# Linear attention: one norm for the outputs of two chunks, and a scaling by two factors

## The chip, the cores and the metric

The kernel runs on one core of a Trainium2 chip. The metric is the device time of one execution in microseconds. Engines are named as in the profile: PE (TensorE) multiplies matrices, DVE (VectorE) and ACT (ScalarE) work element by element, POOL (GpSimd) makes masks, and SP (SyncE) issues nearly all transfers.

## The reference, cut to what matters

One layer of a decoder step: a shared input projection, a stick-breaking attention group, a gated linear attention group, SiLU gates, an output projection and residual norms, for a prompt of 16 + 1024 tokens and 8 samples of 4 tokens with paged keys and values. The change lies in the linear attention group, whose output of 256 columns per head is normed by token before its gate:

```python
def rms_norm(x, g):
    xf = x.astype(jnp.float32)
    var = jnp.mean(xf * xf, axis=-1, keepdims=True)
    return (xf * lax.rsqrt(var + EPS) * g.astype(jnp.float32)).astype(x.dtype)
...
    o_gla = rms_norm(o_gla, gla_norm_g)
    o_gla = o_gla.transpose(0, 2, 1, 3).reshape(B, L, GLA_WIDTH)
...
    mixed = jnp.concatenate([o_sb * jax.nn.silu(sg), o_gla * jax.nn.silu(gg)], axis=-1)
```

## The kernel before

The input projection is the spine of the program. `inproj` makes 128 columns of it at a time, for all tokens in three pieces, as three matmuls for each of 16 slices (a high and a low half of both operands): `acc_gk` is such a projection, of the keys of a linear attention head. Other work is written as Python generators and woven in: `inproj` calls `W.beat()` after every six matmuls, and a beat lets each generator whose delay has run out (`W.spawn(generator, delay)`, `yield n`) write its next instructions. One beat is about 1 us of matmuls. The tile framework's scheduler then sets each engine's order from this sequence and its own estimates; at run time each engine takes its queue strictly in that order and waits on semaphores.

The four heads ("groups") of the linear attention run in turn, from about 900 to 1460 us. `chunks` goes through nine chunks of 128 tokens (the ninth has 16), two beats apart. For each chunk TensorE makes `U`, the chunk's part of the state, and `o`, its output, partly from the last state `S`; VectorE updates `S`; ScalarE copies `o` to the tile `ow` and squares it, with the row sums in `ssq`. Then `chunk_out` is spawned. It calls `rstd_` for 1/sqrt of the mean square: `v` on VectorE, an estimate `r` by logarithm and exponential on ScalarE, one Newton correction `t` in three VectorE steps, and `r*t` in a fourth. VectorE scales `ow` by that; three beats later TensorE transposes the two halves of `ow` into one PSUM tile `otr`, ScalarE copies each half to `gst` with the norm's gain, and SP writes each to DRAM (`od`) for the gate to read later.

Between these stand, on the same engines: `decay` of the next head (tiles `al`, `ny`, `e`, `cb`; not for the last head), the split of the projection's weights (`wr` to `wh` on ScalarE and `wl` on VectorE), and `z_feed`, the samples' attention logits on VectorE: four `jk` instructions for each page `kp` of cached keys, two beats apart, with pages fetched up to six ahead on SP's queue. SP's queue holds the `od` writes, the pages, and the weights.

The staging tiles (`stage`) rotate over seven buffers, the tiles `U`, `o` and `otr` have one PSUM buffer each, and `ssq` three small ones.

Of the kernel before, what the change touches and what calls it, by code (L numbers as in the profile page):

```python
# [10 lines left out]
F32 = mybir.dt.float32  # L11
# [4 lines left out]
AF = mybir.ActivationFunctionType  # L16
ALU = mybir.AluOpType
# [3 lines left out]
P = 128  # L21
# [12 lines left out]
DV = 256  # L34
# [48 lines left out]
def hybrid_step(ctx: ExitStack, tc: tile.TileContext, x_prompt, x_sample, cache_k, cache_v, state_gla,  # L83
# [5 lines left out]
    vec, act, pool = nc.vector, nc.scalar, nc.gpsimd  # L89
# [17 lines left out]
    W = Weaver()  # L107

    def stage(nm, dt=F32):
        return stg.tile([P, 384], dt, tag="stg", name=nm)  # L110
# [41 lines left out]
    td = [dram.tile([P, 8, 1024], F32, name=f"td{j}") for j in range(4)]  # L152
    sd = [[dram.tile([P, 512], F32, name=f"sd{j}_{k}") for k in range(8)] for j in range(2)]

    def rstd_(pl, ssq, n, rows, w, nm):

        v = pl.tile([P, w], F32, tag="rs_v", name=f"v_{nm}")
        r = pl.tile([P, w], F32, tag="rs_r", name=f"r_{nm}")
        t = pl.tile([P, w], F32, tag="rs_t", name=f"t_{nm}")
        v, r, t = v[:rows], r[:rows], t[:rows]  # L160
        vec.tensor_scalar(v, ssq, 1.0 / n, EPS, ALU.mult, ALU.add)
        act.activation(r, v, AF.Ln)
        act.activation(r, r, AF.Exp, scale=-0.5)
        vec.tensor_tensor(t, r, r, ALU.mult)
        vec.tensor_tensor(t, t, v, ALU.mult)
        vec.tensor_scalar(t, t, -0.5, 1.5, ALU.mult, ALU.add)
        vec.tensor_tensor(r, r, t, ALU.mult)
        return r

# [22 lines left out]
    with tc.tile_pool(name="xp", bufs=2) as xp, tc.tile_pool(name="xps", bufs=5, space=PSUM) as xps:  # L192
# [57 lines left out]
        for c, (lo, hi) in enumerate(CHUNKS):  # L250
            n = hi - lo
# [401 lines left out]
    with tc.tile_pool(name="gp", bufs=1) as gp, tc.tile_pool(name="gps", bufs=1, space=PSUM) as gps:  # L653
# [11 lines left out]
        def view(t, off, *dims):  # L665
            a = t if isinstance(t, bass.AP) else t[:]
            return bass.AP(tensor=a.tensor, offset=a.offset + off, ap=[list(a.ap[0])] + [list(d) for d in dims])

        def col(c):

            return EB * (1 - c % 2) + c // 2 * P

        def slot(c):

            return 8 if c == 8 else 4 * (1 - c % 2) + c // 2
# [204 lines left out]
                yield 1  # L880
                packed(rep, pv[:, f * P:(f + 1) * P], 1, f"v{g}_{f}")

        def chunk_out(g, c, rows, ow, ssq):

            r = rstd_(gp, ssq[:rows], DV, rows, 1, f"g{g}_{c}")
            vec.tensor_scalar(ow[:rows, :DV], ow[:rows, :DV], r, None, ALU.mult)
            yield 3
            ps = gps.tile([P, DV], F32, tag="tr", name=f"otr{g}_{c}")
            st = stage(f"gst{g}_{c}")
            s0 = META if c == 0 else 0  # L890
            for f in range(2):
                nc.tensor.transpose(ps[:, f * P:f * P + rows], ow[:rows, f * P:(f + 1) * P], ident[:rows, :rows])
                src = view(ps, f * P + P - 1, (-1, P)) if c % 2 else ps[:, f * P:f * P + rows]
                act.activation(st[:, f * P:f * P + rows], src, AF.Copy, scale=gnrm[:, f:f + 1])
                nc.sync.dma_start(od[8 + 2 * g + f][:, c * P + s0 - META:c * P + rows - META], st[:, f * P + s0:f * P + rows])

        def samples_out(g, ow, ssq):

            r = rstd_(gp, ssq[:, 0:2], DV, P, 2, f"g{g}_s")
            for i in range(2):  # L900
                vec.tensor_scalar(ow[i], ow[i], r[:, i:i + 1], None, ALU.mult)
            yield 9
            ps = gps.tile([P, 512], F32, tag="tr", name=f"otr{g}_s")
            st = stage(f"gst{g}_s")
            for i in range(2):
                for f in range(2):
                    nc.tensor.transpose(ps[:, (2 * i + f) * P:(2 * i + f + 1) * P], ow[i][:, f * P:(f + 1) * P], ident[:])
            for f in range(2):
                act.activation(view(st, f * NSMP, (16, 2), (NT, 4), (1, NT)), view(ps, f * P, (2 * P, 2), (32, 4), (1, NT)),
                               AF.Copy, scale=gnrm[:, f:f + 1])  # L910
                nc.sync.dma_start(od[8 + 2 * g + f][:, SEQ:TOUT], st[:, f * NSMP:(f + 1) * NSMP])

        def chunks(g, at, qt, gv, pv, res):

            kd, ebl, pk = res["kd"], res["ebl"], res["pk"]
            S = None
            Ss = {}

            def load_state(b):
                Ss[b] = gp.tile([P, DV], F32, tag="Sb", bufs=4, name=f"Sb{g}_{b}")  # L920
                nc.sync.dma_start(Ss[b][:], state_gla[0, b, g])

            for c in range(9):
                last = c == 8
                rows = 16 if last else P
                ow = stage(f"ow{g}_{c}")
                ssq = gp.tile([P, 2], F32, tag="ssq", bufs=3, name=f"gssq{g}_{c}")
                U = gps.tile([P, DV], F32, tag="U", name=f"U{g}_{c}")
                for f in range(2):
                    mm(U[:, f * P:(f + 1) * P], kd[:rows, c * P:(c + 1) * P], gv[f][:rows, c * P:(c + 1) * P], start=True, stop=True)  # L930
                o = gps.tile([P, DV], F32, tag="o", name=f"o{g}_{c}")
                for f in range(2):
                    oh = o[:rows, f * P:(f + 1) * P]
                    mm(oh, at[:rows, slot(c), :rows], gv[f][:rows, c * P:(c + 1) * P], start=True, stop=(S is None))
                    if S is not None:
                        mm(oh, qt[:, col(c):col(c) + rows], S[:, f * P:(f + 1) * P], start=False, stop=True)
                Sn = gp.tile([P, DV], F32, tag="S", bufs=2, name=f"S{g}_{c}")
                if S is None:
                    act.copy(Sn[:], U[:])
                else:  # L940
                    vec.scalar_tensor_tensor(Sn[:], S[:], ebl[:, c:c + 1], U[:], ALU.mult, ALU.add)
                S = Sn
                act.copy(ow[:rows, :DV], o[:rows])
                act.activation(o[:rows], ow[:rows, :DV], AF.Square, accum_out=ssq[:rows, 0:1])
                W.spawn(chunk_out(g, c, rows, ow, ssq[:, 0:1]), 1)
                if c in (3, 4, 5, 6):
                    load_state(c - 3)
                yield 2
            nc.sync.dma_start(new_state_prompt[0, 0, g], S[:])

            os_ = gps.tile([P, 2, DV], F32, tag="o", name=f"os{g}")
            for f in range(2):
                for i in range(2):
                    for j in range(4):
                        b = 4 * i + j
                        mm(os_[32 * j:32 * j + 32, i, f * P:(f + 1) * P], at[:48, 8, 16 + NT * b:48 + NT * b],
                           gv[f][:48, 8 * P:9 * P], start=(f == 0 and i == 0), stop=False, skip_group_check=True)
            for b in range(NB):
                if b % 4 == 0:
                    for j in range(4):  # L960
                        n = REAL + NT * (b + j)
                        mm(os_[32 * j:32 * j + 32, b // 4, :], qt[:, n:n + 32], Ss[b + j][:], start=False, stop=True,
                           skip_group_check=True)
                Sb = Ss.pop(b)
                km = stg.tile([96, 384], F32R, tag="stg", name=f"km{g}_{b}")[:, :P]
                vec.tensor_scalar(km, pk[:].bitcast(F32), rmask[:, b:b + 1], None, ALU.mult)
                yield 2
                U = gps.tile([P, DV], F32, tag="U", name=f"Us{g}_{b}")
                mm(U[:], km, pv[:], start=True, stop=True)
                sn = stage(f"sn{g}_{b}")[:, :DV]  # L970
                vec.scalar_tensor_tensor(sn, Sb[:], ebl[:, 9 + b:10 + b], U[:], ALU.mult, ALU.add)
                nc.sync.dma_start(new_state_sample[0, b, g], sn)
                if b + 4 < NB:
                    load_state(b + 4)
            ssq = gp.tile([P, 2], F32, tag="ssq", bufs=3, name=f"gssq{g}_s")
            ow = [stage(f"ow{g}_s{i}")[:, :DV] for i in range(2)]
            for i in range(2):
                act.copy(ow[i], os_[:, i, :])
                act.activation(os_[:, i, :], ow[i], AF.Square, accum_out=ssq[:, i:i + 1])
            W.spawn(samples_out(g, ow, ssq), 1)  # L980
# [7 lines left out]
        for g in range(GH):  # L988
# [30 lines left out]
            if g + 1 < GH:  # L1019
                start_decay(g + 1)  # L1020
            W.spawn(chunks(g, at, qt, gv, pv, res), 4)
        for g in range(3, 5):
            gate_group(g)
# [183 lines left out]
    with ExitStack() as out:  # L1207
# [124 lines left out]
        ssq = op.tile([P, 8, 8], F32, tag="yssq", bufs=1, name="yssq")  # L1332
# [238 lines left out]
```

## Time and profile before

| | |
|---|---|
| runs of the kernel before | 2106.34, 3647.29, 2102.87 us (median 2106.34) |
| profiled execution | 2099.06 us, span 2097.3 us |
| granted TensorE clock over the span | 0.997 |
| instructions in the span | 42175 |
| DMA | 301.87 MB, mean 144 GB/s |

The profile is of one execution. The span goes from its first to its last instruction; the execution's own time is 1.8 us longer. Busy times by engine overlap, so they don't add up to the span. A line number such as L886 is that of the kernel before.

### The profile page before, as it was taken

What the parts mean: (1) busy time and instruction counts of PE and PEld (TensorE: products, weight loads), DVE (VectorE), ACT (ScalarE), POOL (GpSimd) and SP (SyncE); (2) the same over time, 40 slices, a digit from 0 to 9 for tenths busy, and PEclk for the clock granted to TensorE, in tenths of its full rate; (3) what the DMA queues carried; (4) which work ended last, traced back from release to release, by engine and by line L of the source; (5) the groups of instructions that cost most, each with busy time, mean ns of one, the idle gap of its engine ahead of it and who ended that gap; (6) DMA issues with size and microseconds to landing.
All of it is one profiled execution on the core that took longest, in us unless ns stands there. A gap on an engine that the chain in (4) does not pass through costs nothing.

```text
span 2097.3 us, 42175 instructions
## 1 busy us (share of the span) xinstructions
PE 2053.5 (98%) x12546; PEld 1865.4 (89%) x12546; DVE 1561.0 (74%) x6372; ACT 962.4 (46%) x2315; POOL 81.2 (4%) x298
## 2 busy tenths in 40 slices
PE   6999999999999999999999999999999999999998
PEld 4999999999999999999899898998988898777776
DVE  7368888889888989898888888887543347453576
ACT  7345555565655556433525335243433325342342
POOL 0000000101000000020000000000000000000000
PEclk9999999999999999999999999999999999999999
DMA  6255554545555442433332433334766675342485
GB/s 203 82 138 153 137 151 136 168 129 152 146 154 141 141 123 77 142 93 78 100 105 78 117 84 101 98 82 140 248 225 229 223 231 190 131 158 73 131 280 187
DMA packets 374912, 301.87 MB, mean 144 GB/s; under 512 B 46489, under 2 KB 315193, under 8 KB 374681
## 3 DMA queue, kind: packets, MB, share of 16 engines
q1 hardware_dynamic: 372488, 298.90, 47.9%
q8 instruction: 99, 1.62, 0.3%
q14 instruction: 133, 1.08, 0.2%
q10 hardware_dynamic: 2192, 0.27, 0.1%
HBM read 241.75 MB, written 57.31 MB: 143 GB/s over the span
## 4 chain that ended last, share of the span: by engine, by line
PE 85%; DVE 7%; DMA 4%; ACT 2%; issue 2%; SPq 0%; DVEq 0%; ACTq 0%; POOL 0%
PE acc_g L292 6%; PE acc_g L293 6%; PE acc_g L294 6%; PE b L1478 4%; PE b L1479 4%; PE b L1480 4%; PE acc_k L292 3%; PE acc_k L293 3%; PE acc_k L294 3%; PE acc_q L292 3%; PE acc_v L292 3%; PE acc_q L293 3%; PE acc_q L294 3%; PE acc_v L294 3%; PE acc_v L293 3%; PE acc_gv L292 2%
## 5 line engine op out<-in xcount | busy, mean ns | idle before, releaser
L393 DVE SCALAR_TENSOR_TENSOR jk<-kp,qb 128x128 f32<-128x128 f32 x2048 | 592.1, 289 | 42.6 <-DMA qb<-qsd 1.7
L292 PE MATMUL acc_g<-hT,wh_g 128*128 128x368 f32 (+2 forms) x768 | 251.2, 327 | 0.0
L293 PE MATMUL acc_g<-hT,wh_g 128*128 128x368 f32 (+2 forms) x768 | 247.2, 322 | 0.0
L294 PE MATMUL acc_g<-hT,wl_g 128*128 128x368 f32 (+2 forms) x768 | 247.0, 322 | 0.0
L1478 PE MATMUL b<-ring,f 128*128 128x512 f32 x416 | 165.3, 399 | 2.7 <-ACT b L1351 1.4
L1316 DVE TENSOR_TENSOR ring<-wr,ring 128x512 fp32r<-128x512 f32 x104 | 70.6, 690 | 129.9 <-ACT ring L1315 129.7
L393 DVE DVE_READ_ACCUMULATOR jk<-kp,qb 128x1 f32 x2048 | 166.3, 81 | 0.0
L1479 PE MATMUL b<-ring,f 128*128 128x512 f32 x416 | 162.6, 391 | 0.7 <-DVE ring L1316 0.7
L1480 PE MATMUL b<-ring,f 128*128 128x512 f32 x416 | 162.2, 390 | 0.0
L292 PEld LDWEIGHTS acc_g<-hT,wh_g 128*128 128x128 f32 x768 | 144.3, 188 | 12.3 <-issue 10.6
L293 PEld LDWEIGHTS acc_g<-hT,wh_g 128*128 128x128 f32 x768 | 144.5, 188 | 0.7
L294 PEld LDWEIGHTS acc_g<-hT,wl_g 128*128 128x128 f32 x768 | 144.3, 188 | 0.8 <-issue 0.8
L1315 ACT CAST ring<-wr 128x512 fp32r<-128x512 f32 x104 | 64.4, 621 | 157.3 <-DMA wr<-in_w_out_dram 74.9
L292 PE MATMUL acc_gv<-hT,wh_gv 128*128 128x384 f32 (+1 forms) x384 | 129.9, 338 | 0.0
L292 PE MATMUL acc_k<-hT,wh_k 128*128 128x378 f32 (+1 forms) x384 | 127.6, 332 | 0.0
L293 PE MATMUL acc_k<-hT,wh_k 128*128 128x378 f32 (+1 forms) x384 | 125.4, 326 | 0.0
L292 PE MATMUL acc_q<-hT,wh_q 128*128 128x368 f32 (+2 forms) x384 | 125.3, 326 | 0.0
L294 PE MATMUL acc_k<-hT,wl_k 128*128 128x378 f32 (+1 forms) x384 | 125.2, 326 | 0.0
L294 PE MATMUL acc_gv<-hT,wl_gv 128*128 128x384 f32 (+1 forms) x384 | 124.6, 325 | 0.0
L293 PE MATMUL acc_gv<-hT,wh_gv 128*128 128x384 f32 (+1 forms) x384 | 124.5, 324 | 0.0
L293 PE MATMUL acc_q<-hT,wh_q 128*128 128x368 f32 (+2 forms) x384 | 123.6, 322 | 0.0
L294 PE MATMUL acc_q<-hT,wl_q 128*128 128x368 f32 (+2 forms) x384 | 123.5, 322 | 0.0
(441 smaller groups left out, 5314.5 us busy)
## 6 DMA issues: line engine op xcount, KB each, us to landing
kp<-in_cache_k_dram SPq DMA_DIRECT2D x512, 64.0 KB
vr<-in_cache_v_dram SPq DMA_DIRECT2D x64, 512.0 KB
tf<-in_w_out_dram SPq DMA_DIRECT2D x64, 256.0 KB
td<-tf SPq DMA_DIRECT2D x64, 256.0 KB
qb<-qsd SPq DMA_DIRECT2D x64, 256.0 KB
wr_g<-in_w_in_dram SPq DMA_DIRECT2D x64, 256.0 KB
wr<-td SPq DMA_DIRECT2D x64, 256.0 KB
wr<-in_w_out_dram SPq DMA_DIRECT2D x48, 256.0 KB
```

What stands on the lines that cost most here:

```text
L292: mm(acc[c][:, :n], wh, hh[k][:, lo:hi], start=(k == 0), stop=False)
L293: mm(acc[c][:, :n], wh, hl[k][:, lo:hi], start=False, stop=False)
L294: W.mark = mm(acc[c][:, :n], wl, hh[k][:, lo:hi], start=False, stop=(k == NK - 1)).ins
L393: ins = vec.scalar_tensor_tensor(jk[:], kp[:], 1.0, qbs[h, b][:, t, :], ALU.mult, ALU.mult, accum_out=zt[:, t, NPG - 1 - i:NPG - i])
L1315: act.copy(wh, r)
L1316: vec.tensor_tensor(wl, r, wh.bitcast(F32), ALU.subtract)
L1478: mm(bk[:], ah, wh, start=first and k == 0, stop=False, skip_group_check=True)
L1479: mm(bk[:], ah, wl, start=False, stop=False, skip_group_check=True)
L1480: mm(bk[:], al, wh, start=False, stop=last and k == 7, skip_group_check=True)
```

## The change

The generator `chunk_out` becomes two functions. The sums of squares of an even chunk and the odd one after it lie side by side in one `ssq` tile. After the odd chunk (and after the ninth, alone) `chunks_out` is spawned: `rstd_` works on both columns at once, and hands back its estimate `r` and correction `t` without multiplying them. Each chunk's `ow` is scaled by both in one instruction. Two beats later the even chunk's transposes, copies and writes are written, and two beats after that the odd one's; they stood three beats after each chunk's own scaling.

```diff
-    def rstd_(pl, ssq, n, rows, w, nm):
+    def rstd_(pl, ssq, n, rows, w, nm, parts=False):
...
         vec.tensor_scalar(t, t, -0.5, 1.5, ALU.mult, ALU.add)
+        if parts:
+            return r, t
         vec.tensor_tensor(r, r, t, ALU.mult)
         return r
...
-        def chunk_out(g, c, rows, ow, ssq):
-
-            r = rstd_(gp, ssq[:rows], DV, rows, 1, f"g{g}_{c}")
-            vec.tensor_scalar(ow[:rows, :DV], ow[:rows, :DV], r, None, ALU.mult)
-            yield 3
+        def chunks_out(g, group, ssq):
+
+            rows, n = group[0][1], len(group)
+            r, t = rstd_(gp, ssq[:rows, :n], DV, rows, n, f"g{g}_{group[0][0]}", True)
+            for i, (c, _, ow) in enumerate(group):
+                vec.tensor_scalar(ow[:rows, :DV], ow[:rows, :DV], r[:, i:i + 1], t[:, i:i + 1], ALU.mult, ALU.mult)
+            for c, _, ow in group:
+                yield 2
+                chunk_out(g, c, rows, ow)
+
+        def chunk_out(g, c, rows, ow):
+
             ps = gps.tile([P, DV], F32, tag="tr", name=f"otr{g}_{c}")
...
-                ssq = gp.tile([P, 2], F32, tag="ssq", bufs=3, name=f"gssq{g}_{c}")
+                if c % 2 == 0:
+                    ssq, group = gp.tile([P, 2], F32, tag="ssq", bufs=3, name=f"gssq{g}_{c}"), []
+                group.append((c, rows, ow))
...
-                act.activation(o[:rows], ow[:rows, :DV], AF.Square, accum_out=ssq[:rows, 0:1])
-                W.spawn(chunk_out(g, c, rows, ow, ssq[:, 0:1]), 1)
+                act.activation(o[:rows], ow[:rows, :DV], AF.Square, accum_out=ssq[:rows, c % 2:c % 2 + 1])
+                if c % 2 or last:
+                    W.spawn(chunks_out(g, group, ssq), 1)
```

The scheduler moves other instructions around this. Names in the rows below end in the chunk's number and a buffer's; all are of the first group. Line numbers of the changed kernel differ by a few.

On TensorE, before, from the first transpose of chunk 0 (`otr_0`) to the projection after chunk 2:

```order
L892 MATMUL otr_0_17624<-ident,ow_0_17495 128x128
L930 MATMUL U_2_17634<-gv_0_16389,kd_17336 128x128
L930 MATMUL U_2_17634<-gv_1_16877,kd_17336 128x128
L934 MATMUL o_2_17637<-gv_0_16389,at_16386 128x128
L892 MATMUL otr_0_17624<-ident,ow_0_17495 128x128
L936 MATMUL o_2_17637<-S_1_17571,gq_15971 128x128
L934 MATMUL o_2_17637<-gv_1_16877,at_16386 128x128
L936 MATMUL o_2_17637<-S_1_17571,gq_15971 128x128
L292 MATMUL acc_gk_2_17404<-hT_150,wh_gk_1_17577 128x304
```

And with the change, from the end of chunk 2's output on:

```order
L947 MATMUL o_2_17617<-S_1_17559,gq_15971 128x128
L294 MATMUL acc_gk_2_17404<-hT_150,wh_gk_1_17565 128x304
L295 MATMUL acc_gk_2_17404<-hT_150,wh_gk_1_17565 128x304
L296 MATMUL acc_gk_2_17404<-hT_150,wl_gk_1_17566 128x304
L294 MATMUL acc_gk_2_17404<-hT_151,wh_gk_1_17565 128x304
L295 MATMUL acc_gk_2_17404<-hT_151,wh_gk_1_17565 128x304
L296 MATMUL acc_gk_2_17404<-hT_151,wl_gk_1_17566 128x304
L901 MATMUL otr_0_17652<-ident,ow_0_17495 128x128
L294 MATMUL acc_gk_0_17402<-hT_152,wh_gk_1_17565 128x384
L295 MATMUL acc_gk_0_17402<-hT_152,wh_gk_1_17565 128x384
L296 MATMUL acc_gk_0_17402<-hT_152,wl_gk_1_17566 128x384
L901 MATMUL otr_0_17652<-ident,ow_0_17495 128x128
```

The two transposes of chunk 0 moved from ahead of and within chunk 2's matmuls to six projection matmuls behind them, and three matmuls stand between them.

On VectorE, before, chunk 0's norm from its first step to the scaling:

```order
L161 TENSOR_SCALAR v_g_0_17532<-gssq_0_17496 128x1
L393 SCALAR_TENSOR_TENSOR jk_5_6_1_17526,zt_5_17250<-kp_5_6_17277,qb_5_17034 128x128
L393 SCALAR_TENSOR_TENSOR jk_5_6_2_17528,zt_5_17250<-kp_5_6_17277,qb_5_17034 128x128
L164 TENSOR_TENSOR t_g_0_17534<-r_g_0_17533 128x1
L393 SCALAR_TENSOR_TENSOR jk_5_6_3_17530,zt_5_17250<-kp_5_6_17277,qb_5_17034 128x128
L165 TENSOR_TENSOR t_g_0_17534<-t_g_0_17534,v_g_0_17532 128x1
L166 TENSOR_SCALAR t_g_0_17534<-t_g_0_17534 128x1
L167 TENSOR_TENSOR r_g_0_17533<-r_g_0_17533,t_g_0_17534 128x1
L886 TENSOR_SCALAR ow_0_17495<-ow_0_17495,r_g_0_17533 128x256
```

And with the change, the norm of chunks 0 and 1, and what stands ahead of it:

```order
L747 TENSOR_TENSOR e_0_17541<-ny_0_17540,e_0_17541 128x384
L395 SCALAR_TENSOR_TENSOR jk_5_7_2_17590,zt_5_17250<-kp_5_7_17308,qb_5_17034 128x128
L753 SCALAR_TENSOR_TENSOR cb_17400<-ones,e_0_17541 128x128 x3
L395 SCALAR_TENSOR_TENSOR jk_5_7_3_17592,zt_5_17250<-kp_5_7_17308,qb_5_17034 128x128
L161 TENSOR_SCALAR v_g_0_17595<-gssq_0_17496 128x2
L952 SCALAR_TENSOR_TENSOR S_2_17622<-S_1_17559,ebl_17195,U_2_17614 128x256
L164 TENSOR_TENSOR t_g_0_17597<-r_g_0_17596 128x2
L165 TENSOR_TENSOR t_g_0_17597<-t_g_0_17597,v_g_0_17595 128x2
L166 TENSOR_SCALAR t_g_0_17597<-t_g_0_17597 128x2
L890 TENSOR_SCALAR ow_0_17495<-ow_0_17495,r_g_0_17596,t_g_0_17597 128x256
L890 TENSOR_SCALAR ow_1_17550<-ow_1_17550,r_g_0_17596,t_g_0_17597 128x256
```

The norm's first step moved behind the decay's maximum (`e_0`), its three scans (`cb`) and the page's last `jk`, and the update of `S_2` stands between it and the correction.

On ScalarE, before, around the copies of chunk 2's transposes (`gst_2`):

```order
L894 ACTIVATE gst_2_17768<-otr_2_17767,gnrm 128x128
L943 COPY ow_4_17775<-o_4_17780 128x256
L743 ACTIVATE e_1_17758<-e_1_17758 128x384
L894 ACTIVATE gst_2_17768<-otr_2_17767,gnrm 128x128
L744 ACTIVATE e_1_17758<-e_1_17758 128x384
L944 ACTIVATE o_4_17780,gssq_4_17776<-ow_4_17775 128x256
```

And with the change:

```order
L954 COPY ow_4_17743<-o_4_17748 128x256
L745 ACTIVATE e_1_17734<-e_1_17734 128x384
L955 ACTIVATE o_4_17748,gssq_4_17744<-ow_4_17743 128x256
L746 ACTIVATE e_1_17734<-e_1_17734 128x384
L903 ACTIVATE gst_2_17791<-otr_2_17790,gnrm 128x128 x2
```

The copies moved behind the decay's exponential and logarithm (`e_1`) and the square of chunk 4, and stand together.

## The prediction

> **What bounds the kernel now.** I read the page first: busy time by engine, the 40 slices, and the chain that ended last.
>
> ```profile
> span 2097.3 us, 42175 instructions
> PE 2053.5 (98%) x12546; PEld 1865.4 (89%) x12546; DVE 1561.0 (74%) x6372; ACT 962.4 (46%) x2315; POOL 81.2 (4%) x298
> PE   6999999999999999999999999999999999999998
> DVE  7368888889888989898888888887543347453576
> PE 85%; DVE 7%; DMA 4%; ACT 2%; issue 2%; SPq 0%; DVEq 0%; ACTq 0%; POOL 0%
> ```
>
> TensorE is busy in 2053.5 of 2097.3 us. All that could be won by freeing other engines is its idle time, 2097.3 - 2053.5 = 43.8 us, which is 2.1% of the span, and that is spread over the whole program. Then the stretches in which the four groups' chunk outputs are made, as busy time by stage, and what TensorE waits for from 980 to 1460 us.
>
> ```profile
> 998.70:1031.30 32.60, 32.60 (x232) 30.71 (x231) 28.14 (x151) 22.48 (x74) 0.00 (x0) 1.00 0.31 84
> 1128.50:1161.20 32.70, 32.70 (x237) 30.82 (x238) 28.16 (x153) 22.48 (x75) 0.00 (x0) 1.00 0.30 84
> 1258.30:1291.00 32.70, 32.70 (x234) 30.82 (x233) 27.88 (x152) 22.25 (x74) 0.00 (x0) 1.00 0.31 84
> 1388.40:1419.90 31.50, 31.50 (x229) 29.93 (x227) 22.03 (x135) 19.03 (x64) 0.00 (x0) 1.00 0.35 87
> PE os L962 <- DMA Sb<-in_state_gla_dram: 1.0, 1, 1.0
> PE tr_v L867 <- DVE pk L859: 0.6, 3, 0.3
> ```
>
> The columns are the stretch, its length, then busy time of PE, weight loads, VectorE, ScalarE. TensorE has no gap in any of the four; VectorE is at 28.14 of 32.60 us (86%), in the last at 22.03 of 31.50 (70%). In 480 us the view lists 1.6 us of waits on TensorE, none of them for the scaled output `ow`. So work taken off VectorE or ScalarE here buys nothing by itself; the change can only cost, where it makes `ow` late for the transposes, which stand in TensorE's queue ahead of projection matmuls.
>
> **What is removed.** The steps of one norm, from the groups by tile (count, then least, median and greatest ns):
>
> ```profile
> L161 DVE TENSOR_SCALAR v_g<-gssq x36: 142/153/155, 1000.9 to 1418.9; 128x1 f32<-128x1 f32 x32, 16x1 f32<-16x1 f32 x4
> L162 ACT ACTIVATE r_g<-v_g x36: 183/203/207, 1001.1 to 1419.1; 128x1 f32<-128x1 f32 x32, 16x1 f32<-16x1 f32 x4
> L167 DVE TENSOR_TENSOR r_g<-r_g,t_g x36: 141/159/160, 1002.2 to 1420.2; 128x1 f32<-128x1 f32 x32, 16x1 f32<-16x1 f32 x4
> L886 DVE TENSOR_SCALAR ow<-ow,r_g x36: 334/353/356, 1002.4 to 1420.5; 128x256 f32<-128x256 f32 x32, 16x256 f32<-16x256 f32 x4
> L167 DVE TENSOR_TENSOR r_g_s<-r_g_s,t_g_s x4: 156/157/157, 1057.8 to 1447.6; 128x2 f32<-128x2 f32 x4
> L941 DVE SCALAR_TENSOR_TENSOR S<-S,ebl,U x32: 468/474/481, 1003.9 to 1416.5; 128x256 f32<-128x256 f32 x32
> ```
>
> Nine norms a group become five (four pairs and the last chunk). Per group that is 4 x 4 small VectorE steps fewer (v, t, t, t) and 9 fewer of L167: 25, in four groups 100; at 0.155 us they are 15.5 us. ScalarE loses 4 x 2 x 4 = 32 steps of 0.203 us, 6.5 us. A step two columns wide costs what one column does (157 against 159 ns), so pairing adds nothing. The scaling by two factors is not in this trace. It lies between L886 with one factor (0.353) and L941, which reads two tensors and a factor (0.474); 36 x 0.12 = 4.3 us if it were the latter. I take 0.353, the same kind of instruction. On VectorE the balance is -11 to -15.5 us, and all of it goes to the end at nothing: the projection matmuls cover it. If that cover were gone, 15.5 us would be 0.7%.
>
> **What is moved.** An even chunk's norm now starts only when the odd chunk's sum of squares is there, and its transposes move by one beat (about 1 us). Whether TensorE waits is worked out on the first pair of the first group, from the times in order of the three engines. I quote the old places and lay the new order over their spacing.
>
> ```profile
> 1003.87 0.53 ACT L743 ACTIVATE e<-e 128x384 f32<-128x384 f32 x1 [0.16 <-DVE e L742]
> 1004.30 0.37 ACT L944 ACTIVATE o<-ow 128x256 f32<-128x256 f32 x1
> 1004.70 0.51 ACT L744 ACTIVATE e<-e 128x384 f32<-128x384 f32 x1
> 1005.23 0.27 PE L892 MATMUL otr<-ident,ow 128*128 128x128 f32 x1
> 1005.24 0.56 DVE L745 TENSOR_TENSOR e<-ny,e 128x384 f32<-128x384 f32 x1
> 1005.34 0.61 PE L930 MATMUL U<-gv,kd 128*128 128x128 f32 x4
> 1005.60 0.37 ACT L894 ACTIVATE gst<-otr,gnrm 128x128 f32<-128x128 f32 x1
> 1005.72 0.28 DVE L393 SCALAR_TENSOR_TENSOR jk<-kp,qb 128x128 f32<-128x128 f32 x1
> 1005.78 0.39 PE L934 MATMUL o<-gv,at 128*128 128x128 f32 x2
> 1005.93 1.05 DVE L751 TENSOR_TENSOR_SCAN cb<-ones,e 128x128 f32<-128x128 f32 x3
> 1006.02 0.33 PE L892 MATMUL otr<-ident,ow 128*128 128x128 f32 x1
> 1006.18 0.39 PE L936 MATMUL o<-S,gq 128*128 128x128 f32 x2
> 1006.77 0.39 PE L292 MATMUL acc_gk<-hT,wh_gk 128*128 128x304 f32 x1
> 1006.90 0.13 DVE L164 TENSOR_TENSOR t_g<-r_g 128x1 f32<-128x1 f32 x1
> 1006.95 0.47 DVE L941 SCALAR_TENSOR_TENSOR S<-S,ebl,U 128x256 f32<-128x256 f32 x1
> 1007.52 0.15 DVE L166 TENSOR_SCALAR t_g<-t_g 128x1 f32<-128x1 f32 x1
> 1007.69 0.34 PE L292 MATMUL acc_gk<-hT,wh_gk 128*128 128x384 f32 x1
> 1007.90 0.35 DVE L886 TENSOR_SCALAR ow<-ow,r_g 128x256 f32<-128x256 f32 x1
> ```
>
> When TensorE wants it: without the transpose of 1005.23 the matmuls of U start there; U takes 0.44 (1005.34 to 1005.78), the output matmuls 0.99 less the 0.16 of the transpose among them (1005.78 to 1006.77), the six `acc_gk` 0.92 (1006.77 to 1007.69). 1005.23 + 0.44 + 0.83 + 0.92 = 1007.42: there stands the first transpose now.
>
> When it is ready: VectorE now has the maximum of the decay (L745 before), a `jk`, three scans and a `jk` ahead of the norm's first step. L745 waits for ScalarE's logarithm (1004.70 + 0.51). In the new order the square comes behind that logarithm, which may so come earlier by one ScalarE step (1004.70 - 1004.30 = 0.40), or not. Earliest 1004.84. From there by the old spacing: 0.48 to the `jk`, 0.21 to the scans, 0.97 to their end, 0.33 for the second `jk` with its hand-over: the norm's first step at +1.99. That step and the two on ScalarE take 0.15 + 2 x 0.20, with three hand-overs about 0.67, an estimate, while S passes; then three steps of 0.19 (1007.52 to 1007.90 is two) and the scaling's 0.35. 1004.84 + 1.99 + 0.67 + 0.57 + 0.35 = 1008.42. TensorE waits 1.0 us, with the later logarithm 1.4. Bounds: nothing, if the queue is 1 us quicker than its old spacing, and 1.5. I take 1.0. What waits behind it are the `acc_gk` matmuls of every projection, so it is time on the path.
>
> Second halves: the second transpose must wait for ScalarE's copy of the first, 1006.02 - 1005.23 = 0.79 after it. Now only three matmuls stand between for chunks 0 and 3 (0.11 + 3 x 0.17 = 0.63, wait 0.16), four for 1 and 4 (0.75, wait 0.04): 0.4 us a group. For chunks 2 and 5 the copy stands on ScalarE behind the decay's exponential and logarithm (0.53, 0.51): 0.2 each, 0.4 a group. For chunk 6 the scaling stands behind the next group's level steps on VectorE: 0.3. Sum for a group: 1.0 + 0.4 + 0.4 + 0.3 = 2.1 us, bounds 0 and 4. The last group has no decay ahead and a VectorE with 30% room; I take 0.4 there. Total 3 x 2.1 + 0.4 = 6.7 us. Today's waits could shrink, by 1.6 us at most as the rows above have it; I leave that out of the sum.
>
> The moved writes of the outputs go past `kp` loads on SP's queue. Their cover is that pages are asked for six ahead, each worth four `jk` of 0.28 and four reads of their sums:
>
> ```profile
> L393 DVE DVE_READ_ACCUMULATOR jk<-kp,qb 128x1 f32 x2048 | 166.3, 81 | 0.0
> ```
>
> 4 x 0.36 = 1.4 us a page, and over 8 us in six. I price this at nothing; the third rival says what it costs without that cover.
>
> **The sum.** The profiled execution took 2099.06 us (span 2097.3). 2099.06 + 6.7 = 2105.8. The undisturbed runs shown are 2102.87 and 2106.34 (the latter the median), 3.8 and 7.3 above the profiled one; +6.7 on their middle, 2104.6, gives 2111. I predict **2111 us**, 0.2% over the median: no change that can be told. About 2% is what a measurement of this kernel can tell.
>
> **Rivals.** *The waits do not arise* (0.26). VectorE is freed of 3.9 us a group, and if its queue gains on TensorE by more than the 1 us that the moved norm needs, the transposes find `ow` ready, as all do today. Against: what is freed lies partly behind the new place. Time: 2104.6 less the waits of 1.6 us, 2103.
>
> *TensorE loses its clock* (0.04), the slower side. The trace has one wait that was followed by half speed:
>
> ```profile
> 908.28 0.44 PE L292 MATMUL acc_gq<-hT,wh_gq 128*128 128x384 f32 x1 [2.64 <-ACT gk L681]
> 909.49 0.53 PE L294 MATMUL acc_gq<-hT,wl_gq 128*128 128x384 f32 x1
> 909.81 0.53 PE L292 MATMUL acc_gq<-hT,wh_gq 128*128 128x384 f32 x1
> 905.00:930.00 25.00, 21.52 (x124) 20.77 (x123) 24.04 (x119) 8.64 (x17) 2.22 (x4) 0.93 0.30 83
> ```
>
> After 2.64 us of waiting matmuls start 0.32 apart instead of 0.17, and the granted clock of the stretch is 0.93: 7% of 25 us, 1.7 us. If each of the twelve pairs of three groups waited so long, it would be 12 x (2.64 + 1.7) = 52 us: 2157. It decides from 2.6 us a pair; my longest wait is 1.5. [...]
>
> *SP's queue holds the pages* (0.08). A `kp` load behind a late output write would stop VectorE for a page (1.4 us) in each of twelve pairs, and S and `ow` behind it: 17 us more, 2128. For it: the writes wait for ScalarE's copies. Against: the lead of six pages.
>
> **How the numbers follow.** Forecast 0.62, rivals 0.26, 0.04, 0.08. Faster by over 2% needs nearly all of TensorE's 43.8 us: 0.01, for what I do not see. Slower by over 2% is the clock's case and a little of the queue's: 0.05. Within 2%: 0.94. The range goes from the first rival less the runs' spread (the profiled one lay 5.5 us under their middle) to the third rival with the runs' spread above: 2098 to 2131 us.
>
> **What would show it.** Right: `PE otr` waiting for VectorE's `ow` at the first chunk of pairs in three groups, about 1 us each, and no such wait in the last group; stretches of the four groups 1 to 4 us longer; 100 VectorE and 32 ScalarE steps gone; the scaling at 0.35. Wrong: no waits at all; a granted clock below 1 in those stretches; `jk` waiting for `kp`; or a scaling near 0.47.

## The result and the profile after

The changed kernel takes 2112.08 us, the median of 7 runs (2108.31 to 2116.33); the kernel before takes 2106.15, the median of 7. The ratio is 1.0034, with a 95% interval of 1.0019 to 1.0049: about 7 us slower (4 to 10). One of the seven runs before took 3647.29 us; the ratio leaves it out. Forecast were 2111 us and a difference below 2%. The profiled execution took 2116.33 us, the longest of the seven.

The page's first lines after, and the chain that ended last by engine:

```profile
span 2114.6 us, 42018 instructions
PE 2064.1 (98%) x12546; PEld 1867.7 (88%) x12546; DVE 1555.5 (74%) x6272; ACT 956.1 (45%) x2283; POOL 80.5 (4%) x298
PE 82%; DVE 8%; DMA 5%; ACT 2%; issue 2%; SPq 0%; DVEq 0%; ACTq 0%; POOL 0%
```

VectorE has 6372 - 6272 = 100 steps fewer and ScalarE 2315 - 2283 = 32, as worked out, yet the span is 17.3 us longer than that of before. Not all of this belongs to the change: where the first group begins, the order of the instructions is still the same on every engine, and the trace is 5.26 us behind there already. Profiled executions differ by that much by themselves (in the first-group rows below this group begins anywhere from 997.06 to 1003.96), so the comparison has to be made group by group. Each row below is one group, from a projection matmul ahead of its first chunk to one behind its samples; the ends are chosen so that both kernels have the same matmuls between them (425, 427, 429, 490). The columns are the stretch, its length, busy time and count of PE, weight loads, VectorE, ScalarE, GpSimd, then the granted clock, DMA share and GB/s. Before:

```profile
998.70:1060.00 61.30, 61.30 (x425) 55.45 (x425) 53.23 (x275) 32.45 (x101) 0.23 (x2) 1.00 0.36 101
1128.50:1190.00 61.50, 61.50 (x427) 55.68 (x427) 53.32 (x278) 32.41 (x101) 0.24 (x2) 1.00 0.37 101
1258.30:1320.00 61.70, 61.70 (x429) 55.89 (x429) 53.23 (x278) 32.22 (x100) 0.24 (x2) 1.00 0.36 102
1388.40:1460.00 71.60, 70.64 (x490) 64.76 (x489) 55.64 (x308) 35.44 (x106) 0.58 (x2) 1.00 0.44 121
```

and after:

```profile
1003.96:1066.98 63.02, 62.43 (x425) 54.94 (x425) 51.06 (x249) 30.92 (x93) 0.24 (x2) 1.00 0.35 98
1135.49:1198.78 63.29, 62.70 (x427) 55.23 (x427) 51.23 (x252) 30.93 (x93) 0.24 (x2) 1.00 0.35 98
1267.09:1330.83 63.74, 62.98 (x429) 55.43 (x429) 51.10 (x252) 30.75 (x92) 0.24 (x2) 1.00 0.35 98
1399.50:1473.85 74.35, 72.59 (x490) 64.83 (x489) 52.61 (x272) 33.55 (x97) 0.37 (x2) 0.98 0.40 114
```

VectorE is busy some 2.1 us less in each of the first three groups, and TensorE takes 1.72, 1.79, 2.04 and 2.75 us longer: 8.30 us together. This fits the 7 us of the timed runs. TensorE's waits in the four groups:

```profile
PE os L974 <- DMA Sb<-in_state_gla_dram: 1.9, 2, 1.8
PE otr L901 <- DVE ow L890: 1.8, 3, 0.6
PE tr_v L869 <- DVE pk L861: 1.0, 4, 0.6
```

The second row was not there before: three waits of 0.6 us for `ow`, one in each of the first three groups. The first row was there with 1.0 us; it comes back below.

The first pair of the first group, in order of time, from all engines:

```profile
1009.27 0.53 ACT L746 ACTIVATE e<-e 128x384 f32<-128x384 f32 x1
1009.83 0.56 DVE L747 TENSOR_TENSOR e<-ny,e 128x384 f32<-128x384 f32 x1 [0.22 <-ACT e L746]
1010.52 1.05 DVE L753 TENSOR_TENSOR_SCAN cb<-ones,e 128x128 f32<-128x128 f32 x3
1011.68 0.16 DVE L161 TENSOR_SCALAR v_g<-gssq 128x2 f32<-128x2 f32 x1
1012.35 0.16 DVE L164 TENSOR_TENSOR t_g<-r_g 128x2 f32<-128x2 f32 x1
1012.53 0.30 PE L296 MATMUL acc_gk<-hT,wl_gk 128*128 128x304 f32 x1
1012.94 0.74 DVE L890 TENSOR_SCALAR ow<-ow,r_g,t_g 128x256 f32<-128x256 f32 x2
1013.41 0.33 PE L901 MATMUL otr<-ident,ow 128*128 128x128 f32 x1 [0.59 <-DVE ow L890]
1013.93 0.34 PE L296 MATMUL acc_gk<-hT,wl_gk 128*128 128x384 f32 x1
1014.20 0.33 PE L901 MATMUL otr<-ident,ow 128*128 128x128 f32 x1
```

The norm's first step stands behind the decay's scans, as the order of the program said. TensorE's last matmul ahead of the transpose starts at 1012.53; these narrower matmuls start 0.14 apart, so the transpose was due at 1012.67 and starts at 1013.41: 0.74 us lost from start to start. Two steps of the norm by tile, with least, median and greatest ns:

```profile
L890 DVE TENSOR_SCALAR ow<-ow,r_g,t_g x36: 396/408/416, 1012.9 to 1432.1; 128x256 f32<-128x256 f32 x32, 16x256 f32<-16x256 f32 x4
L161 DVE TENSOR_SCALAR v_g<-gssq x20: 136/169/172, 1011.7 to 1430.5; 128x2 f32<-128x2 f32 x16, 16x1 f32<-16x1 f32 x4
```

The scaling by two factors takes 0.408 us where that by one took 0.353.

### The profile page after: what moved, and what is told of

Its sections match the earlier page's. It is cut to its first block, busy times and chain, and to the rows that moved or that the text cites. A ratio compares the mean times of both kernels' runs of the same rounds, so it can differ in the third digit from the quotient of the medians.

```text
span 2114.6 us, 42018 instructions
## 1 busy us (share of the span) xinstructions
PE 2064.1 (98%) x12546; PEld 1867.7 (88%) x12546; DVE 1555.5 (74%) x6272; ACT 956.1 (45%) x2283; POOL 80.5 (4%) x298
## 4 chain that ended last, share of the span: by engine, by line
PE 82%; DVE 8%; DMA 5%; ACT 2%; issue 2%; SPq 0%; DVEq 0%; ACTq 0%; POOL 0%
PE acc_g L294 5%; PE acc_g L295 5%; PE acc_g L296 5%; PE b L1490 4%; PE b L1491 4%; PE b L1492 4%; PE acc_k L294 3%; PE acc_k L295 3%; PE acc_k L296 3%; PE acc_v L294 3%; PE acc_q L294 3%; PE acc_q L295 3%; PE acc_q L296 3%; PE acc_v L295 3%; PE acc_v L296 3%; PE acc_gv L294 2%
```

## The experiments

The theory (A): the loss comes from where the paired norm and its transposes stand, and nothing comes back for the steps saved. The rivals are in each expectation. Every ratio below is to the kernel before, run on the same chip.

### The two halves of the change

The scaling by two factors alone, each chunk with its own norm and at its old place:

```diff
-            r = rstd_(gp, ssq[:rows], DV, rows, 1, f"g{g}_{c}")
-            vec.tensor_scalar(ow[:rows, :DV], ow[:rows, :DV], r, None, ALU.mult)
+            r, t = rstd_(gp, ssq[:rows], DV, rows, 1, f"g{g}_{c}", True)
+            vec.tensor_scalar(ow[:rows, :DV], ow[:rows, :DV], r, t, ALU.mult, ALU.mult)
```

(`rstd_` has the flag `parts` as in the change.)

> The scaling by two factors alone: each chunk has its own norm as before, only r*t is left out and the scaling takes r and t. Theory A (the loss comes from where the paired norm and the transposes stand): the order of the transposes is that of before, TensorE waits nowhere for ow, VectorE has 36 steps fewer and each scaling takes 0.41 instead of 0.35 us; time within 1 us of before, ratio 1.000. Rival B (the loss comes with the form of the scaling): ratio 1.002 to 1.0035.

Measured: 0.9994 (0.9985 to 1.0003). Its first and last group:

```profile
1002.80:1063.92 61.12, 61.05 (x425) 55.26 (x425) 52.22 (x266) 32.76 (x101) 0.24 (x2) 1.00 0.39 102
1392.23:1464.72 72.49, 70.94 (x490) 64.77 (x489) 54.92 (x296) 35.92 (x106) 0.81 (x3) 1.00 0.43 119
```

The first group is 0.18 us shorter than before, with 1.0 us less work on VectorE. The form of the scaling cost nothing, and the microsecond saved on VectorE bought less than 0.2 here. The pairing alone, with `r*t` multiplied out:

```diff
-            r, t = rstd_(gp, ssq[:rows, :n], DV, rows, n, f"g{g}_{group[0][0]}", True)
+            r = rstd_(gp, ssq[:rows, :n], DV, rows, n, f"g{g}_{group[0][0]}")
...
-                vec.tensor_scalar(ow[:rows, :DV], ow[:rows, :DV], r[:, i:i + 1], t[:, i:i + 1], ALU.mult, ALU.mult)
+                vec.tensor_scalar(ow[:rows, :DV], ow[:rows, :DV], r[:, i:i + 1], None, ALU.mult)
```

> The pairing alone: r*t is multiplied out for two columns, the scaling takes one factor. Theory A: like the whole change, ratio 1.003 to 1.004. ow comes 0.19 later for the added step and 0.06 earlier for the shorter scaling, the transposes stand one matmul (0.17) later: TensorE waits about 0.7 us for ow at the first pair of groups 0 to 2. Rival B: ratio 1.000 to 1.001.

Measured: 1.0031 (1.0019 to 1.0043). Its first group:

```profile
1001.49:1064.52 63.03, 62.39 (x425) 54.86 (x425) 51.45 (x255) 31.14 (x93) 0.24 (x2) 1.00 0.35 99
```

and TensorE's waits for `ow` in its four groups:

```profile
PE otr L901 <- DVE ow L890: 1.7, 3, 0.6
```

63.03 against 63.02 with the whole change: the loss is the pairing's. Rival B falls.

### The transposes a beat later

```diff
-            for c, _, ow in group:
-                yield 2
+            for i, (c, _, ow) in enumerate(group):
+                yield 3 if i == 0 else 2
```

> The whole change, with the even chunk's transposes asked for three beats after the scaling instead of two (the odd one's follow two beats behind): in the first pair they move six projection matmuls (1 us) further down. Theory A: the waits of 0.75 us at the first pair of three groups go, 2.2 us; what the second halves and the last group cost stays: ratio 1.002 to 1.0025. Rival C (the wait only moves on, to the copies or to the staging buffers, which are held a beat longer): ratio 1.0034 or more, with longer waits of km and of the sample states.

Measured: 0.9999 (0.9990 to 1.0008). Its first and last group:

```profile
1001.33:1062.70 61.37, 61.37 (x425) 55.42 (x425) 50.99 (x250) 31.45 (x93) 0.24 (x2) 1.00 0.36 100
1391.56:1463.52 71.96, 70.75 (x490) 64.85 (x489) 53.63 (x279) 33.56 (x96) 0.71 (x3) 1.00 0.42 120
```

The whole loss is gone, 1.65 us in the first group where 0.75 was expected, so theory A's ratio is missed too. Of rival C's waits one came, 1.2 us for ScalarE's copy in the last group; a wait for a sample state is no longer listed. VectorE still has its 100 steps fewer, and still nothing is won by them. That more came back than the wait for `ow` has to do with the order: a beat later chunk 0's transposes stand at the matmuls of `U` and `o` again, as they did before, with six matmuls between the two halves instead of three. What that is worth, the next run shows.

### The places alone

The kernel before, unpaired, with its transposes a beat later, so that they stand between projection matmuls nearly where the change puts them, while every `ow` is ready early:

```diff
-            yield 3
+            yield 4
```

> The kernel before, not paired, with the transposes asked for four beats after each chunk's scaling instead of three. TensorE's order in the chunks of the groups is then nearly that of the whole change (transposes between projection matmuls, three or four matmuls between the two halves), while each chunk has its norm as early as before. Theory A, with two parts (the late norm costs 0.75 us at the first pair of three groups; the places among the projections cost 0.6 to 0.7 us a group, whoever fills them): no wait for ow, the chunks' stretches 0.6 to 0.7 us longer than before, the last group's samples as with the whole change; ratio 1.002 to 1.0025. Rival N (everything comes from the late norm): ratio 1.000, no stretch longer.

Measured: 1.0015 (1.0004 to 1.0025). No wait for `ow` is listed. Its first group:

```profile
997.06:1059.24 62.18, 62.18 (x425) 54.97 (x425) 53.84 (x277) 32.05 (x101) 0.23 (x2) 1.00 0.37 100
```

0.88 us longer than before, without any gap on TensorE. The remaining 63.02 - 62.18 = 0.84 us of the change is then, by difference, the late norm. (The second and third group of this run hold waits of 1.2 and 1.7 us for the samples' states, so the first is the one to compare.) Rival N falls. One part of theory A falls with it: the last group's samples did not lose as with the whole change, that group is only 0.20 us longer.

Where the 0.88 us lie can be read from the starts of the matmuls. Chunk 0's two transposes in this run:

```profile
1005.63 0.30 PE L294 MATMUL acc_gk<-hT,wl_gk 128*128 128x304 f32 x1
1005.77 0.27 PE L892 MATMUL otr<-ident,ow 128*128 128x128 f32 x1
1005.79 0.42 PE L292 MATMUL acc_gk<-hT,wh_gk 128*128 128x384 f32 x1
1006.05 0.33 PE L293 MATMUL acc_gk<-hT,wh_gk 128*128 128x384 f32 x1
1006.22 0.33 PE L294 MATMUL acc_gk<-hT,wl_gk 128*128 128x384 f32 x1
1006.50 0.33 PE L892 MATMUL otr<-ident,ow 128*128 128x128 f32 x1
1006.58 0.42 PE L292 MATMUL acc_gk<-hT,wh_gk 128*128 128x384 f32 x1
1006.84 0.34 PE L293 MATMUL acc_gk<-hT,wh_gk 128*128 128x384 f32 x1
```

In these traces the matmul behind one of 304 columns usually starts 0.14 later, behind one of 384 columns 0.17. The first transpose adds 1006.05 - 1005.63 - 0.14 - 0.17 = 0.11 us, no more than the one ahead of the narrow matmuls of `U` in the kernel before (1005.23 to 1005.34 in the prediction's rows). The second adds 1006.84 - 1006.22 - 2 x 0.17 = 0.28. Its weight load waits for ScalarE's copy of the first half, as such loads do 33 times in the four groups of this run and 4 times (0.8 us) before:

```profile
PEld otr L892 <- ACT gst L894: 7.8, 33, 0.3
```

Counted in this way over the first group, the second halves cost 0.69 us more than before and the first halves 0.07 less; the other 0.26 lie in the rest of the matmuls. So most of the price of these places is the wait of the second halves for the copy. In the first group of the whole change the second halves cost 0.67 more than before, chunk 0's first transpose 0.81 (the late norm), the rest 0.24.

The other way round, the whole change with one beat between a chunk's two transposes:

```diff
-                chunk_out(g, c, rows, ow)
+                yield from chunk_out(g, c, rows, ow)
...
             for f in range(2):
+                if f:
+                    yield 1
                 nc.tensor.transpose(...)
```

> The whole change, with one beat between a chunk's two transposes, so that the second stands at least six matmuls behind the first and ScalarE's copy is done by then. Theory H (the second halves wait for the copy, 0.4 + 0.4 us a group by the prediction): these waits go, about 0.8 us a group, the first pair's wait of 0.75 us stays; ratio 1.002. Rival S (the second halves cost only the change from a projection matmul to a transpose and back, which the kernel before pays too at some places): stretches within 0.2 us of the whole change's, ratio 1.003 to 1.0035.

Measured: 1.0018 (1.0007 to 1.0028). Its first group:

```profile
1000.87:1062.68 61.81, 61.12 (x425) 54.91 (x425) 51.54 (x249) 30.51 (x93) 0.24 (x2) 1.00 0.37 101
```

and chunk 1's second transpose, which now stands between projection matmuls with six of them between it and the first:

```profile
1017.34 0.34 PE L296 MATMUL acc_gk<-hT,wl_gk 128*128 128x384 f32 x1
1017.51 0.27 PE L903 MATMUL otr<-ident,ow 128*128 128x128 f32 x1
1017.54 0.42 PE L294 MATMUL acc_gk<-hT,wh_gk 128*128 128x384 f32 x1
1017.80 0.34 PE L295 MATMUL acc_gk<-hT,wh_gk 128*128 128x384 f32 x1
```

The waits for `ow` are as long as with the change (three, 1.8 us), and the group is 1.21 us shorter: theory H said 0.8, rival S at most 0.2. The second half in these rows waits for nothing and adds 1017.80 - 1017.34 - 2 x 0.17 = 0.12 us, so this transpose between projection matmuls costs by itself about what the first one ahead of `U` did before (0.11), and rival S falls. Of the weight loads' waits for the copy 10 are left in the four groups (2.5 us) of 29 (7.2 us) with the change. The size is not H's alone: over the first group the second halves cost 1.23 us less than with the change, but the first halves 0.66 more, and the other matmuls 0.62 less.

### The last group's samples

In the last group the chunks lose 0.48 us and the samples 2.27. (The cut between the two is where the matmuls of the samples begin; three matmuls have moved across it. Counted by matmul, the transposes cost 0.55 us more and the rest 2.2.) Three transfers of SP's queue and the matmul that waits, from the timeline of the change:

```profile
1443.53 0.43 SPq L372 DMA_DIRECT2D qb<-qsd  x1
1444.45 0.39 SPq L181 DMA_DIRECT2D wr_g<-in_w_in_dram  x1
1446.10 0.45 SPq L930 DMA_DIRECT2D Sb<-in_state_gla_dram  x1
1451.19 0.62 PE L974 MATMUL os<-Sb,gq 128*32 128x256 f32 x2 [1.76 <-DMA Sb<-in_state_gla_dram]
```

and two stretches there by their windows:

```profile
1449.00:1451.20 2.20, 0.44 (x5) 0.20 (x3) 0.69 (x5) 0.62 (x1) 0.00 (x0) 1.00 1.08 372
1453.00:1456.00 3.00, 3.00 (x10) 1.75 (x9) 1.16 (x8) 0.00 (x0) 0.00 (x0) 0.50 0.52 153
```

TensorE needs the state that SP asked for at 1446.10 and has it 5.1 us later, while the DMA engines are full (share 1.08, 372 GB/s); it waits 1.76 us, and from 1453 to 1456 its granted clock is one half, by estimate worth 1.5 us more. The wait for a state was 1.0 before, and no such spell followed (granted clock 1.00 from 1441 to 1460): 1.76 - 1.0 + 1.5 = 2.3 us. VectorE had waited 1.9 us for a staging buffer that a late `od` write held (`km` for `od<-gst`), which looked like the cause. So `km` got buffers of its own:

```diff
-                km = stg.tile([96, 384], F32R, tag="stg", name=f"km{g}_{b}")[:, :P]
+                km = gp.tile([96, P], F32R, tag="km", bufs=2, name=f"km{g}_{b}")
```

> The whole change, with the samples' masked keys km in two buffers of their own, no longer in the ring of seven staging buffers. Theory R (in the last group the late writes of the outputs hold staging buffers, km waits 1.9 us for one, and through the state loads TensorE 1.8 us): VectorE no longer waits for an od write, TensorE's wait for the sample states falls to 1.0 us or less, the stretch of the last group's samples is about 2 us shorter; ratio 1.0022 to 1.0027. Rival Q (the state loads stand behind the four od writes and a page in SP's queue, whatever km does): TensorE's wait of 1.8 us stays, ratio 1.0034.

Measured: 1.0033 (1.0019 to 1.0046). The wait of `km` for a write went, another of 2.5 us for the matmul of `Us` took its place, and TensorE waited longer for the state:

```profile
PE os L974 <- DMA Sb<-in_state_gla_dram: 2.2, 1, 2.2
```

Theory R falls; the wait stays, as rival Q had it. Then a fifth buffer for the states, in the change and in the kernel with the later transposes:

```diff
-                Ss[b] = gp.tile([P, DV], F32, tag="Sb", bufs=4, name=f"Sb{g}_{b}")
+                Ss[b] = gp.tile([P, DV], F32, tag="Sb", bufs=5, name=f"Sb{g}_{b}")
...
-                if c in (3, 4, 5, 6):
-                    load_state(c - 3)
+                if c in (2, 3, 4, 5, 6):
+                    load_state(c - 2)
...
-                if b + 4 < NB:
-                    load_state(b + 4)
+                if b + 5 < NB:
+                    load_state(b + 5)
```

> The whole change, with five buffers instead of four for the samples' states Sb, so that a fifth state is loaded ahead of the samples and each later one is asked for one sample earlier. Theory L (2 us of the loss lie in the last group's samples, where TensorE waits 1.8 us for a state and then runs some 3 us at half clock): the wait for Sb falls below 1 us and no half-clock spell follows it; the rest of the change's loss (late norm 0.8 us in three groups, places 0.5 us in four) stays; ratio 1.0022 to 1.0027. Rival O (the wait was of that one execution): ratio 1.0034, as for the whole change.

> Both remedies: the even chunk's transposes a beat later as in the run with the later transposes, and five buffers for the states. Theory A with L: no wait of TensorE for ow or for Sb in the groups; 1 us less than the later transposes alone, ratio 0.9985 to 0.9999, hardly apart from 1. Rival C (a wait in its place, as ScalarE's copy of 1.2 us in the last group was with the later transposes): ratio 1.000 to 1.001.

Measured: 1.0032 (1.0020 to 1.0045) for the change with it, 0.9996 (0.9986 to 1.0005) with the later transposes as well. The first one's TensorE waits 1.9 us for a state. The last group of the second:

```profile
1391.08:1461.92 70.84, 70.62 (x490) 64.87 (x489) 53.54 (x279) 33.42 (x96) 0.71 (x3) 1.00 0.43 120
```

With the change one buffer more does not help; a later state is waited for instead. Theory L falls, and so does rival O's reason, since the wait came again in another execution. With the transposes a beat later the last group is 0.76 us shorter than before, but the ratio holds 1 in its interval: this is no version that beats the kernel before by what can be measured. Last, the late state loads from ScalarE's queue:

```diff
-            def load_state(b):
+            def load_state(b, q=nc.sync):
...
-                nc.sync.dma_start(Ss[b][:], state_gla[0, b, g])
+                q.dma_start(Ss[b][:], state_gla[0, b, g])
...
-                    load_state(b + 4)
+                    load_state(b + 4, nc.scalar)
```

> The whole change, with the late state loads (samples 4 to 7 of each group) issued from ScalarE's queue instead of SP's, where in the last group they stand behind a 256 KB load of projection weights and one of 256 KB of queries. Theory F (the load that TensorE waits for lands 5 us after its issue because it runs behind those two transfers of the same queue): it lands in 3 us or less, TensorE's wait for Sb falls below 0.7 us, no half-clock spell follows, the last group's samples lose 2 us less; ratio 1.0022 to 1.0027. Rival D (the DMA engines are full then, whatever queue the load is in): the wait stays between 1 and 2 us, ratio 1.003 to 1.0035.

Measured: 1.0079 (1.0065 to 1.0092), slower than either theory said. Now the first three groups wait too. TensorE's waits for a state:

```profile
PE os L974 <- DMA Sb<-in_state_gla_dram: 7.7, 4, 2.4
```

and the first group:

```profile
998.21:1064.54 66.33, 64.03 (x425) 56.02 (x425) 51.31 (x249) 30.85 (x93) 0.24 (x2) 0.97 0.34 95
```

Here the clock fell too (0.97). The loads are not issued late: in the second group the one that is waited for is issued at 1178.99, as soon as its buffer is free (the `sn` that reads the old state ends at 1178.95), and used at 1185.19, 6.2 us later. In the last group the load was issued at 1449.08 and used at 1453.1, after a wait of 1.43 us. Theory F falls; rival D's wait holds in the last group, its ratio does not. What makes the states late was not settled. It came and went from edit to edit: the last group's surplus over before was 2.75 us with the change, 2.67 with the pairing alone, 3.16 and 3.08 in the two attempts to mend it, 0.89 with the factors alone, 0.36 with the later transposes and 0.20 with the places alone.

### All runs side by side

| | ratio | four groups, us over before |
|---|---|---|
| the change | 1.0034 | 8.30 |
| two factors alone | 0.9994 | 0.36 |
| pairing alone | 1.0031 | 8.10 |
| transposes later | 0.9999 | 0.61 |
| places alone | 1.0015 | 5.95 |
| `km` apart | 1.0033 | 8.35 |
| halves apart | 1.0018 | 5.35 |
| five states | 1.0032 | 8.44 |
| later, five states | 0.9996 | -0.50 |
| states on ScalarE's queue | 1.0079 | 14.86 |

The right column is the sum over the four group stretches of each trace, less 256.10 before. With the halves apart, 3.83 of the 5.35 us lie in the third group, where TensorE waits 1.80 us for a state and then loses its clock for some 3 us (0.50 from 1317 to 1319). The ratios, times 2105 us, follow it within 3 us: what the timed runs show arises in these stretches.

## Why the prediction was right

**What bounds.** TensorE had no gap in the first three groups (busy in all of 61.30, 61.50 and 61.70 us) and 0.96 us of idle time in the last, so freed steps had hardly anything to buy. The factors alone (1.0 us less VectorE work in the first group, 0.18 us won) and the later transposes (all 100 steps saved, 0.9999) show it.

**The wait at the first pair.** Put at 1.0 us, in three groups, none in the last: three waits, 0.74 us from start to start, none in the last. Less the 5.26 us by which this trace is behind, the transpose is due at 1012.67 - 5.26 = 1007.41 (worked out: 1007.42) and starts at 1008.15 (worked out: ready at 1008.42). The whole error is at the start of that chain: the decay's maximum begins at 1009.83 - 5.26 = 1004.57, not 1004.84, since ScalarE's logarithm moved up by more than the 0.40 allowed for it: from 1004.70 to 1009.27 - 5.26 = 1004.01. The spacing behind it was as estimated. The run with the places alone puts the late norm at 0.84.

**Second halves and the rest of a group.** Put at 0.4 + 0.4 + 0.3 = 1.1 us, measured 0.88 with the places alone and 63.02 - 61.30 - 0.81 = 0.91 with the change, of which 0.67 are the second halves. The mechanism is the one worked out, the wait for ScalarE's copy, although TensorE's own waits don't list it, only those of its weight loads (29 times, 7.2 us, with the change). In chunk 0 the second transpose stands 0.79 us behind the first (1013.41 to 1014.20), as worked out. The sizes by chunk are not as put: four matmuls in chunk 1 leave a wait as well, since they are narrower ones that follow one another after 0.14 us. A group was put at 2.1 and cost 1.72, 1.79 and 2.04.

**The last group.** Put at 0.4 us; its chunks cost 0.48. Its samples cost 2.27 more, for which the sum had no term. That is the term that the sum lacked. It moved the sum of 6.7 only to 8.3, because the first three groups were put at 6.3 and cost 5.55; that the total came so near is in part luck. The third rival looked at SP's queue for the pages alone, and the trace of before had the row that mattered: `os` waiting 1.0 us for `Sb`.

**The scaling.** Taken at 0.353, with 0.474 as the other bound: 0.408. 36 x 0.055 = 2.0 us more VectorE work, hidden.

**The rivals.** The waits arose. TensorE kept its clock in all pairs (1.00 in the first three groups' rows). No page held VectorE up: no `jk` is listed with a wait for `kp` from 1000 to 1475. (One wait of 2.4 us in the last group's samples is put down to a `kp`, but it is that of `sn`, which starts at 1452.17, when the matmul of `Us` ends (1452.13).) But the point from which the clock falls, 2.6 us, was read from one wait and is wrong: the clock stood at 0.50 after a wait of 1.76. That is taken up last. And that a measurement of this kernel can tell only some 2% was too cautious: the intervals above are 0.2 to 0.3% wide.

## What to carry to other kernels

Where one engine is full, count for each edit on the others only when its results are ready, and lay that beside the moment at which the full engine's queue asks for them: the 15.5 us of steps saved here were worth nothing, and the 0.74 us by which the first pair came late was paid in full. Look at the waits of weight loads beside those of the matmuls: the copies that held up the second transposes show only there. A paired step starts when its later half is ready, so its consumers have to move by as much; one beat more did it. And when an order moves, read the waits of before for those that have no slack, the loads too: a wait of 1.0 us nearby became 1.8, and 3 us at half clock followed.

## What was not expected of the hardware

Between wide projection matmuls a transpose whose weight load waited for nothing added 0.11 us to TensorE's stream (chunk 0's first with the places alone) or 0.12 (chunk 1's second with the halves apart): in their rows the matmul behind it starts 0.02 to 0.03 us after it, and the next one 0.26 later instead of 0.17. Ahead of the narrow matmuls of `U` in the kernel before it was 0.11. Where the load waited for a copy, it added 0.25 to 0.31 (the first six second halves with the places alone), and TensorE shows no gap for it (busy in 62.18 of 62.18 us).

TensorE's clock fell to one half after a wait of 1.76 us (0.50 from 1453 to 1456 with the change), and in another run it did not after 2.35 (1.00). That second wait, from the timeline of the run with the states on ScalarE's queue:

```profile
1319.31 0.62 PE L974 MATMUL os<-Sb,gq 128*32 128x256 f32 x2 [2.35 <-DMA Sb<-in_state_gla_dram]
```

and the windows of it and of what follows:

```profile
1316.00:1319.50 3.50, 1.15 (x8) 0.86 (x7) 1.32 (x8) 0.00 (x0) 0.00 (x0) 1.00 0.69 211
1319.50:1322.00 2.50, 2.50 (x15) 2.05 (x14) 1.09 (x6) 0.00 (x0) 0.00 (x0) 1.00 0.39 120
```

In the first group of the same run it fell after 1.71 us: the wait ends at 1049.77, and matmuls of 384 columns start 0.32 apart at 1051.60 and 1051.92 instead of 0.17. So there is no one length from which it falls in these traces; what decides it, no run shows.
